# A gate product in 2x2 blocks with seven block products, its weight sums by DMA in DRAM and its operand sums by DMA in place

## The chip, the cores and the metric

The kernel runs on one core of a Trainium2 chip. The metric is the device time of one execution in microseconds, given as the median of three runs. The engines are TensorE (PE, its weight loads PEld), VectorE (DVE), ScalarE (ACT), GpSimd (POOL) and SyncE (SP); SP issues most transfers, POOL the rest, among them all transfers that add to their destination.

## What is computed

One decoder layer on 1024 tokens of width 1024 in float32. Its last two steps matter here, and the sums around them:

```python
h = h + jnp.concatenate([y_a, y_b, y_c], axis=-1) @ w_out[i]
f = jnp.square(jax.nn.relu(rms_norm(h, norm2_g[i]) @ w_ff1[i]))
h = h + f @ w_ff2[i]                                   # FF2, depth 4096
gate = jax.nn.sigmoid(rms_norm(h, norm3_g[i]) @ w_ple_gate[i])   # 1024 x 1024
h = h + gate * (p[i] @ w_ple_proj[i])
```

rms_norm multiplies by the gain g and by one root per token, R = (mean of h squared + eps)^-0.5. The kernel multiplies by g3 before the gate product and by R behind it.

## The kernel before

Activations lie with features on the 128 partitions and tokens along the free axis: h is 8 blocks n of 128 features by two halves h of 512 tokens (`h_res[n][h]`). Every float32 operand is split into a high and a low part (`split` L131 to L138: ScalarE writes hi, VectorE the rest lo), and a product of a 128 x 128 weight unit with 512 token columns is three matmuls, hi by hi, hi by lo, lo by hi (`product` L157 to L163, `run` L727).

FF1 and FF2 already go by the seven-product scheme: weights and activations are 2 x 2 blocks, A11 to A22 of the weight times B11 to B22 of (features, tokens), and products 1 to 7 use single blocks or sums of blocks on both sides. The table for the weight side (L703):

```python
OPERAND = {1: "A11", 2: "A12", 4: "A22", 5: "S1", 6: "S2", 7: "S3", 3: "S4"}
```

The sums S1 to S4 of w_ff2 are made ahead in DRAM (`w_sums`, `block_sums` L282 to L300) by copies and accumulating transfers of POOL. The sums of f are made on POOL by `token_sums` (L721) during FF1, stored in `f_dram`, and fetched again as `f` pairs.

FF2 (L919 to L998) runs over two depth chunks c, in each over the products p in the order `DOWN`, in each product over four blocks j of 128 outputs. One such step is 8 depth units x 3 = 24 matmuls into one PSUM bank; a bank is shared by the mates 1 and 2, 5 and 3, 7 and 4. VectorE then adds the bank to `u_sum` or to `h_res`. In the last chunk `finish` squares a finished h (`late_squares` L783, ScalarE) and POOL adds the squares to `S3[h]`.

The root of a half: `root_of` (L794) multiplies S3 by ones (`ms_ps`), VectorE makes the mean `ms`, POOL the power `r`, VectorE the diagonal `diag`; `spread_root` (L811) multiplies by ones (`R_ps`) and ScalarE copies R into S3's place.

The gate product (L999 to L1034) is plain. Between FF2 and it, `h3` pairs are made from h x g3 by `split`. It runs over pairs of output blocks n0, n0+1; in each pair over half 1 and then half 0; each of the 16 combinations is 8 depth units x 3 matmuls of 512 columns, the last (n = 7, half 0) in two pieces of 256. `gated` (L1006 to L1014) then does four operations on a result: multiply by R (VectorE, from PSUM), sigmoid (ScalarE), multiply by the projected embedding `pps` and add h (both VectorE), and the store: on POOL for n under 6, on SP for 6 and 7. Half 1's root is computed at the start of the gate, half 0's behind the first half-0 block.

PSUM has eight banks; the late SBUF slots are w 22, raw 4, sum 6, tmp 12, R 2 and a pool of 56 slots for h, f, u and pairs. `fetch` (L673) loads on SP. Within an engine instructions are in order; the framework's scheduler sets that order from a simulated timeline, starting from the order in which the program writes them.

Of the kernel before, what the change touches and what calls it, by code (L numbers as in the profile page):

```python
# [7 lines left out]
F32 = mybir.dt.float32  # L8
# [5 lines left out]
P = 128  # L14
# [18 lines left out]
def hybrid_block(ctx: ExitStack, tc: tile.TileContext, a: dict):  # L33
# [687 lines left out]
    def token_sums(b11, b12, b21, b22, eng, t1, t2, t3, t4):  # L721
        subtract(eng, t1, b11, b12)
        add(eng, t2, b22, t1)
        subtract(eng, t3, b22, b12)
        subtract(eng, t4, t2, b21)

    def run(bank, w, b, first, last):  # L727

# [141 lines left out]
    for i in range(FT):  # L870
        slots = iter(range(7 * i, 7 * i + 7))

        def product_up(bank, p, first, last):
            slot_no = next(slots)
            run(bank, up_pairs.pop((i, p)), hn[p], first, last)
            supply(slot_no + 1)
            if stores:
                to, t = stores.pop(0)
                nc.sync.dma_start(to, t)

        ba, bb, bc, bd = (late_bank("f_ps") for _ in range(4))
        product_up(ba, 1, True, False)
        v = late_slot("tmp", "v")
        nc.scalar.copy(v, ba)  # L884
# [27 lines left out]
        token_sums(f11, f12, f21, f22, nc.gpsimd, t1, t2, t3, t4)  # L912
        stores += [(f_dram[i, p - 1], t) for p, t in
                   ((3, f22), (1, f11), (2, f21), (5, t1), (6, t2), (7, t3), (4, t4))]
    for to, t in stores:
        nc.sync.dma_start(to, t)


    h_res = [[None, None] for _ in range(KT)]  # L919
    u_sum = [None] * 4  # L920
    h3 = [[None, None] for _ in range(KT)]
    S3 = [late_slot("R", "S3") for _ in range(2)]
    R3 = S3
    DOWN = (1, 5, 2, 3, 6, 7, 4)
    CHUNKS = FT // KC
    steps = [(c, p, j) for c in range(CHUNKS) for p in DOWN for j in range(4)]

    def f_pairs():
        for c in range(CHUNKS):
            for p in DOWN:  # L930
# [30 lines left out]
    def finish(n, h):  # L961
        late_squares(S3[h], h_res[n][h], not seen[h])
        seen[h] = True

    seen = [False, False]
    for s, (c, p, j) in enumerate(steps):
        bank = d_bank.pop((MATE[p], j)) if p in MATE else late_bank("d_ps")
        if p in (1, 5, 7):
            d_bank[p, j] = bank
        w_of.append(next(w_made, None))  # L970
        make_f(KC // 4)
        run(bank, w_of.pop(0), f_of[c, p], p not in MATE, p not in (1, 5, 7))
        last = c == CHUNKS - 1
        if p == 1:
            if c == 0:
                u_sum[j] = slot("u")
                nc.scalar.copy(u_sum[j], bank)
            else:
                add(nc.vector, u_sum[j], u_sum[j], bank)
        elif p == 6:  # L980
            subtract(nc.vector, u_sum[j], u_sum[j], bank)
            if last:
                add(nc.vector, h_res[j][1], h_res[j][1], u_sum[j])
                finish(j, 1)
                for h in range(2):
                    t = residual(j + 4, h)
                    subtract(nc.vector, t, t, u_sum[j])
        elif p in (2, 3):
            t = residual(j, p - 2)
            add(nc.vector, t, t, bank)  # L990
            if last and p == 2:
                finish(j, 0)
        else:
            h = 0 if p == 4 else 1
            t = residual(j + 4, h)
            subtract(nc.vector, t, t, bank)
            if last and p != 5:
                finish(j + 4, h)  # L998
    for n, h in [(j + 4 * i, h) for i, h in ((0, 0), (0, 1), (1, 1), (1, 0)) for j in range(4)]:  # L999
        h3[n][h] = pair("h3")  # L1000
        split(h_res[n][h], *h3[n][h], scale=g3[:, n:n + 1])


    diag = root_of(S3[1], "31")

    def gated(n, h, g_ps, c):  # L1006
        gt = late_slot("tmp", "gt")[:, c]
        nc.vector.tensor_tensor(out=gt, in0=g_ps, in1=R3[h][:, c], op=ALU.mult)
        nc.scalar.activation(gt, gt, AF.Sigmoid)
        nc.vector.tensor_tensor(out=gt, in0=gt, in1=pps[n, h][:, c], op=ALU.mult)  # L1010
        ot = late_slot("tmp", "ot")[:, c]
        nc.vector.tensor_tensor(out=ot, in0=gt, in1=h_res[n][h][:, c], op=ALU.add)
        queue = nc.sync if n >= KT - 2 else nc.gpsimd
        queue.dma_start(a["out"][n * P:(n + 1) * P, half[h]][:, c], ot)  # L1014

    pps, undone = {}, []
    for n0 in range(0, KT, 2):
        wus = [plain_units(a["w_ple_gate"][n]) for n in (n0, n0 + 1)]
        for n, h in [(n, h) for h in (1, 0) for n in (n0, n0 + 1)]:
            pps[n, h] = fetch(pp_dram[n][:, half[h]], "sum")  # L1020
            last = n == KT - 1 and h == 0

            for c in (slice(0, 256), slice(256, HT)) if last else (slice(0, HT),):
                g_ps = late_bank("g_ps")[:, c]
                product(g_ps, [(wus[n - n0][k], cols(h3[k][h], c)) for k in range(KT)])
                undone.append((n, h, g_ps, c))
                if n == 0:
                    if h == 0:
                        diag = root_of(S3[0], "30")
                    continue  # L1030
                if n == 1:
                    spread_root(diag, R3[h])
                while undone:
                    gated(*undone.pop(0))  # L1034


# [60 lines left out]
```

## Time and profile before

| | |
|---|---|
| runs | 1258.04, 1260.59, 1261.03 us; median 1260.59 |
| profiled execution | 1262.6 us, its span 1260.9 |
| mean granted TensorE clock | 0.984 |
| busy share of the span | PE 96%, PEld 82%, DVE 70%, ACT 48%, POOL 29% |
| FF2, first to last matmul | 860.2 to 1164.8 us |
| gate product | 1165.65 to 1256.06 us |

The times inside the execution count from the start of the span; 1.7 us of the profiled execution lie outside it. Rows of groups have the line, engine, operation, names (out<-in), shape and count, then busy us and mean ns, then idle time before them and what ended it. Rows in order of time begin with start and duration in us; in brackets stands the idle time before and its releaser.

### The profile page before, as it was taken

Reading aid. Unit: us, or ns where it says so; the run is one execution under the profiler, and the core shown is the slowest. Engines: PE = TensorE matmul, PEld = TensorE weight load, DVE = VectorE, ACT = ScalarE, POOL = GpSimd, SP = SyncE. Lnnn points to the kernel's source line nnn. Section 1 sums busy time; section 2 is a strip of 40 time slices with the busy share of each in tenths; the row PEclk is TensorE's granted clock in tenths of the full one; section 3 lists DMA queues with packets and bytes.
Section 4 is the critical chain, followed back from the end, with each engine's and each line's share of the span. In section 5 each row is a group of like instructions: output and inputs, shape, how many; then the busy total and the mean of one; then the engine's idle time right before and its main releaser. Section 6 shows DMA issues by size and latency. Waiting matters only on the chain.

```text
span 1260.9 us, 17509 instructions
## 1 busy us (share of the span) xinstructions
PE 1215.0 (96%) x5868; PEld 1034.1 (82%) x5868; DVE 880.7 (70%) x1324; ACT 603.8 (48%) x1167; POOL 364.2 (29%) x365
## 2 busy tenths in 40 slices
PE   9999898899999999879999999999999999999998
PEld 7898798898888878658888888888888888888887
DVE  7746886898979654676887777777755565686443
ACT  7725655666656454553334334344544344555211
POOL 2324434455323212233553453431000000122110
PEclk9999998999999999989999999999999999999999
DMA  9603257788542298689999999958956565653231
GB/s 309 211 18 117 84 158 210 167 210 159 119 114 38 67 292 226 175 221 251 269 244 255 252 244 250 252 193 302 354 179 224 183 223 170 203 166 106 76 111 51
DMA packets 118700, 234.89 MB, mean 186 GB/s; under 512 B 13105, under 2 KB 20529, under 8 KB 118353
## 3 DMA queue, kind: packets, MB, share of 16 engines
q1 hardware_dynamic: 94752, 168.08, 40.4%
q0 software_dynamic: 23856, 65.70, 23.3%
q8 instruction: 46, 0.75, 0.3%
q14 instruction: 46, 0.37, 0.1%
HBM read 176.57 MB, written 78.64 MB: 202 GB/s over the span
## 4 chain that ended last, share of the span: by engine, by line
PE 82%; DVE 8%; DMA 5%; issue 2%; ACT 1%; POOL 1%; SPq 0%; DVEq 0%; POOLq 0%; ACTq 0%
PE d_ps L731 24%; PE f_ps L731 24%; PE qkv_ps L161 3%; PE qkv_ps L162 3%; PE qkv_ps L163 3%; PE g_ps L161 2%; PE g_ps L163 2%; PE g_ps L162 2%; DVE rem L413 2%; PE av L456 2%; DMA S<-sq 2%; PE w_tr L438 1%; PE cv_ps L161 1%; DMA h_dram<-h 1%; PE cv_ps L162 1%
## 5 line engine op out<-in xcount | busy, mean ns | idle before, releaser
L135 DVE TENSOR_TENSOR w_lo<-raw,w_hi 128x512 fp32r<-128x512 f32 x268 | 244.9, 916 | 94.4 <-ACT w_hi L134 92.2
L134 ACT CAST w_hi<-raw 128x512 fp32r<-128x512 f32 x268 | 165.2, 619 | 242.6 <-PE d_ps L731 116.7
L731 PE MATMUL f_ps<-hn_hi,w_hi 128*128 128x512 f32 x448 | 176.5, 394 | 5.3 <-ACT v L884 5.3
L731 PE MATMUL f_ps<-hn_lo,w_hi 128*128 128x512 f32 x448 | 175.7, 392 | 0.0
L731 PE MATMUL f_ps<-hn_hi,w_lo 128*128 128x512 f32 x448 | 175.3, 392 | 0.0
L731 PE MATMUL d_ps<-f_hi,w_lo 128*128 128x512 f32 x448 | 174.3, 389 | 0.0
L731 PE MATMUL d_ps<-f_hi,w_hi 128*128 128x512 f32 x448 | 174.3, 389 | 0.0
L731 PE MATMUL d_ps<-f_lo,w_hi 128*128 128x512 f32 x448 | 174.3, 389 | 0.0
L731 PEld LDWEIGHTS f_ps<-hn_hi,w_hi 128*128 128x128 f32 x448 | 85.1, 190 | 23.4 <-ACT v L884 5.7
L719 POOL TENSOR_TENSOR S<-S,sq 128x512 f32<-128x512 f32 x14 | 22.6, 1614 | 273.5 <-ACT sq L788 273.5
L731 PEld LDWEIGHTS f_ps<-hn_lo,w_hi 128*128 128x128 f32 x448 | 85.1, 190 | 17.9 <-issue 0.2
L731 PEld LDWEIGHTS f_ps<-hn_hi,w_lo 128*128 128x128 f32 x448 | 85.0, 190 | 18.0
L731 PEld LDWEIGHTS d_ps<-f_hi,w_hi 128*128 128x128 f32 x448 | 84.1, 188 | 17.6
L731 PEld LDWEIGHTS d_ps<-f_lo,w_hi 128*128 128x128 f32 x448 | 84.1, 188 | 17.4
L731 PEld LDWEIGHTS d_ps<-f_hi,w_lo 128*128 128x128 f32 x448 | 84.1, 188 | 17.3
L413 DVE TENSOR_TENSOR_SCAN rem<-rem 128x128 f32<-128x128 f32 (+3 forms) x64 | 89.0, 1393 | 11.1 <-ACT rem L409 10.6
L161 PE MATMUL qkv_ps<-whi,xn_hi 128*128 128x384 f32 x256 | 92.0, 359 | 2.6 <-DVE V L138 2.6
L163 PE MATMUL qkv_ps<-whi,xn_lo 128*128 128x384 f32 x256 | 89.8, 351 | 0.0
L162 PE MATMUL qkv_ps<-wlo,xn_hi 128*128 128x384 f32 x256 | 89.8, 351 | 0.0
L135 DVE TENSOR_TENSOR f_lo<-raw,f_hi 128x512 fp32r<-128x512 f32 x112 | 77.6, 723 | 4.6 <-ACT f_hi L134 4.0
L134 ACT CAST f_hi<-raw 128x512 fp32r<-128x512 f32 x112 | 67.0, 620 | 17.9 <-DMA raw<-f_dram 13.4
L416 POOL TENSOR_TENSOR wt<-wt,rem 128x127 f32<-128x127 f32 (+4 forms) x40 | 44.3, 1109 | 107.7 <-DVE rem L413 44.9
(219 smaller groups left out, 2665.7 us busy)
## 6 DMA issues: line engine op xcount, KB each, us to landing
raw<-in_w_ff SPq DMA_DIRECT2D x160, 256.0 KB, 4.1
raw<-f_dram SPq DMA_DIRECT2D x112, 256.0 KB, 4.8
raw<-w_sums SPq DMA_DIRECT2D x64, 256.0 KB, 3.7
f_dram<-f SPq DMA_DIRECT2D x48, 256.0 KB, 4.4
f_dram<-t SPq DMA_DIRECT2D x48, 256.0 KB, 3.9
w_sums<-in_w_ff POOLq DMA_DIRECT2D x8, 1024.0 KB, 11.7
w_sums<-w_sums POOLq DMA_DIRECT2D x8, 1024.0 KB, 12.4
raw<-in_w_ff POOLq DMA_DIRECT2D x32, 256.0 KB, 5.4
```

The source lines that it names most:

```text
L134: nc.scalar.copy(hi, src)
L135: low.tensor_tensor(out=lo, in0=src, in1=hi, op=ALU.subtract)
L161: nc.tensor.matmul(ps, lh, rh, start=first and i == 0, stop=False)
L162: nc.tensor.matmul(ps, lh, rl, start=False, stop=False)
L163: nc.tensor.matmul(ps, ll, rh, start=False, stop=last and i == len(terms) - 1)
L413: nc.vector.tensor_tensor_scan(out=back, data0=back, data1=back, initial=1.0, op0=ALU.mult, op1=ALU.bypass)
L416: done = (nc.vector if on_vector else nc.gpsimd).tensor_tensor(out=wt[:, :W - 1], in0=wt[:, :W - 1], in1=rem[:, 1:W], op=ALU.mult)
L438: nc.tensor.transpose(tr[:, n:n + P], wts[i][:, kb * P:(kb + 1) * P], ident)
L456: nc.tensor.matmul(av[:, first * P:], lhs, part[:, o:o + m], start=kb == 0 and part is hi, stop=kb == 2 * g + 1 and part is lo)
L719: return eng.tensor_tensor(out=out, in0=x, in1=y, op=ALU.add)
L731: nc.tensor.matmul(bank, l, r, start=first and k == 0 and i == 0, stop=k == len(b) - 1 and i == 2, skip_group_check=True)
```

## The change

1. `w_ple_gate` comes in 2 x 2 blocks (`quad_blocks` on the host, where the arrays are laid out). Its sums S1 to S4 are made in DRAM as `g_sums`: 16 copies and 16 accumulates of 256 KB, all on POOL, behind the last `token_sums` of FF1, that is at the start of FF2.
2. FF2's second chunk takes the products in the order 1, 2, 6, 7, 4, 5, 3. Half 0 is then complete before product 5, and its root is computed inside product 5's steps; half 1 is complete with product 3, the last.
3. The activation side of the gate: for products 1, 2, 3 twelve `h3` pairs straight from h (`h3_pair`). For the sums ScalarE writes 16 scaled copies `hg` (h x g3 or h x -g3, `scale_h`), POOL adds them to each other in place by 16 transfers from SBUF to SBUF (`sum_h`), and `h3_sum` splits the results. Four sums are chained for each block j: 11 += 12, then 12 += 22, then 22 += 11, then 21 += 22, each reading what the one before left.
4. The gate product takes the products in the order 1, 2, 3, 6, 5, 7, 4, four blocks j each, 4 depth units x 3 matmuls a block; the last block of products 7 and 4 in two pieces of 256 columns. Product 2 adds to product 1's banks and 4 to 7's.
5. The epilogue: `gated` as before, with VectorE operations ahead of it for products 6, 5, 7 and 4 (`v`, `e`) and a ScalarE copy of `v` for product 1. Stores go out on POOL but for n = 6 and 7 of half 0, on SP.

```diff
+    minus_g3 = const.tile([P, KT], F32, name="minus_g3")
+    nc.vector.tensor_scalar_mul(minus_g3, g3, -1.0)
...
+    g_sums = dram.tile([4, 4, P, HT], F32, name="g_sums")
+    with tc.issue_after(summed.ins):
+        for j in range(4):
+            for to, what in ((0, "A21"), (2, "A11"), (0, "+A22"), (1, "A11"), (2, "+A21"),
+                             (1, "+S1"), (3, "A12"), (3, "+S2")):
...
+                if what[0] == "+":
+                    nc.gpsimd.dma_start(g_sums[to, j], src, accum_op=ALU.add,
+                                        max_dma_last_dim=2048)
+                else:
+                    nc.gpsimd.dma_start(g_sums[to, j], src)
...
-    DOWN = (1, 5, 2, 3, 6, 7, 4)
+    DOWN = [(1, 5, 2, 3, 6, 7, 4), (1, 2, 6, 7, 4, 5, 3)]
...
+    def scale_h(of, n, h, g):
+        t = scaled[of, n % 4] = slot("hg")
+        nc.scalar.activation(t, h_res[n][h], AF.Copy, scale=g[:, n:n + 1])
...
+    def sum_h(to, of, j):
+        nc.gpsimd.dma_start(scaled[to, j], scaled[of, j], accum_op=ALU.add)
+
+    def h3_sum(p, of, j):
+        h3[p][j] = two_parts(scaled[of, j], lambda s: slot(f"h3_{s}", F32R))
...
+        if last and p == 5:
+            if j == 1:
+                diag = root_of(S3[0], "30")
+            elif j == 3:
+                spread_root(diag, R3[0])
+        elif last and p == 3:
...
+            for n in range(3) if j == 2 else (3,) if j == 3 else ():
+                scale_h("12", n, 1, minus_g3)
+                sum_h("11", "12", n)
...
+    GATE = (1, 2, 3, 6, 5, 7, 4)
+    MATE = {2: 1, 4: 7}
...
+            for bank, c in zip(banks, cs):
+                run(bank, w, [cols(b, c) for b in h3[p]], p not in MATE, p not in (1, 7))
+                if p == 1:
+                    v_of[j] = late_slot("tmp", "v")
+                    nc.scalar.copy(v_of[j], bank)
+                elif p == 2:
+                    gated(j, 0, bank, late_slot("tmp", "gt"), c)
+                elif p == 6:
+                    subtract(nc.vector, v_of[j], v_of[j], bank)
+                elif p == 5:
+                    e_of[j] = late_slot("tmp", "e")
+                    add(nc.vector, e_of[j], bank, v_of[j])
+                    t = late_slot("tmp", "gt")
+                    add(nc.vector, t, d_bank.pop((3, j))[0], e_of[j])
+                    gated(j, 1, t, t, c)
+                elif p == 7:
+                    t = e_of[j][:, c]
+                    add(nc.vector, t, bank, t)
+                    gated(j + 4, 1, t, t, c, -1.0)
+                elif p == 4:
+                    t = v_of[j][:, c]
+                    add(nc.vector, t, bank, t)
+                    gated(j + 4, 0, t, t, c, -1.0)
+            if p == 1:
+                if j == 1:
+                    diag = root_of(S3[1], "31")
+                elif j == 3:
+                    spread_root(diag, R3[1])
+                h3_pair(2, j + 4, 0)
+                sum_h("12", "22", j)
+            elif p == 2:
+                h3_pair(3, j + 4, 1)
+                sum_h("22", "11", j)
+            elif p == 3:
+                h3_sum(6, "22", j)
+                sum_h("21", "22", j)
+            elif p == 6:
+                h3_sum(5, "11", j)
+            elif p == 5:
+                h3_sum(7, "12", j)
+            elif p == 7:
+                h3_sum(4, "21", j)
```

What the change moves shows in the order of instructions on three engines. On POOL, from the end of FF2 on, before: S3 sums of squares, the two roots (L169), and stores.

```order
L719 TENSOR_TENSOR S3_1911_8635<-S3_1911_8635,sq_2627_11353 128x512
L719 TENSOR_TENSOR S3_1910_8634<-S3_1910_8634,sq_2634_11393 128x512
L719 TENSOR_TENSOR S3_1910_8634<-S3_1910_8634,sq_2641_11433 128x512
L719 TENSOR_TENSOR S3_1910_8634<-S3_1910_8634,sq_2648_11473 128x512
L169 TENSOR_TENSOR r_2684_11575<-ms_2683_11573,mhalf_109 128x4
L719 TENSOR_TENSOR S3_1910_8634<-S3_1910_8634,sq_2649_11501 128x512
L1014 DMA out_T<-ot_2704_11664 128x512
L1014 DMA out_T<-ot_2706_11671 128x512
L169 TENSOR_TENSOR r_2711_11708<-ms_2710_11706,mhalf_109 128x4
L1014 DMA out_T<-ot_2717_11746 128x512
L1014 DMA out_T<-ot_2719_11753 128x512
```

And now, the last twelve of the sums in place (L996) with the last sum of squares and half 1's root (L171):

```order
L996 DMA hg_2657_11505<-hg_2676_11571 128x512
L996 DMA hg_2660_11511<-hg_2656_11503 128x512
L721 TENSOR_TENSOR S3_1911_8670<-S3_1911_8670,sq_2677_11599 128x512
L996 DMA hg_2676_11571<-hg_2661_11513 128x512
L996 DMA hg_2658_11507<-hg_2678_11602 128x512
L996 DMA hg_2671_11559<-hg_2660_11511 128x512
L996 DMA hg_2661_11513<-hg_2657_11505 128x512
L171 TENSOR_TENSOR r_2696_11665<-ms_2695_11663,mhalf_109 128x4
L996 DMA hg_2678_11602<-hg_2662_11515 128x512
L996 DMA hg_2672_11561<-hg_2661_11513 128x512
L996 DMA hg_2662_11515<-hg_2658_11507 128x512
L996 DMA hg_2673_11563<-hg_2662_11515 128x512
```

The last sums of squares, which stood side by side, now have transfers between them, and the root r_2696 stands behind the twelfth of sixteen transfers; the stores follow the last.

On TensorE, where half 1's root is spread (R_ps), before: behind the second block of the gate (n = 1), which is complete.

```order
L163 MATMUL g_ps_2701_11632<-h3_hi_2670_11544,w_lo_2697_11600 128x512
L161 MATMUL g_ps_2701_11632<-h3_hi_2672_11548,w_hi_2696_11599 128x512
L162 MATMUL g_ps_2701_11632<-h3_lo_2673_11549,w_hi_2696_11599 128x512
L163 MATMUL g_ps_2701_11632<-h3_hi_2672_11548,w_lo_2697_11600 128x512
L813 MATMUL R_ps_2702_11657<-diag_2685_11577,ones_88 128x512
L161 MATMUL g_ps_2708_11676<-h3_hi_2650_11504,w_hi_2687_11581 128x512
L162 MATMUL g_ps_2708_11676<-h3_lo_2651_11505,w_hi_2687_11581 128x512
```

Now it stands inside the first block of product 2, between its eighth and ninth matmul:

```order
L733 MATMUL g_ps_2682_11611<-h3_lo_2699_11670,w_hi_2709_11703 128x512
L733 MATMUL g_ps_2682_11611<-h3_hi_2698_11669,w_lo_2710_11704 128x512
L733 MATMUL g_ps_2682_11611<-h3_hi_2705_11695,w_hi_2709_11703 128x512
L733 MATMUL g_ps_2682_11611<-h3_lo_2706_11696,w_hi_2709_11703 128x512
L815 MATMUL R_ps_2712_11721<-diag_2697_11667,ones_88 128x512
L733 MATMUL g_ps_2682_11611<-h3_hi_2705_11695,w_lo_2710_11704 128x512
L733 MATMUL g_ps_2682_11611<-h3_hi_2713_11724,w_hi_2709_11703 128x512
L733 MATMUL g_ps_2682_11611<-h3_lo_2714_11725,w_hi_2709_11703 128x512
```

It moved from a place between two blocks, behind 48 matmuls of the gate (two plain blocks of 24), to one inside a block, behind 56.

On VectorE, the end of the program, before: the two pieces of the last block, three operations each (L1008 times R, L1010 times pps, L1012 plus h).

```order
L1008 TENSOR_TENSOR gt_2802_12229<-g_ps_2801_12204,S3_1910_8634 128x256
L1010 TENSOR_TENSOR gt_2802_12229<-gt_2802_12229,raw_2800_12202 128x256
L1012 TENSOR_TENSOR ot_2803_12233<-gt_2802_12229,h_2313_10117 128x256
L1008 TENSOR_TENSOR gt_2805_12261<-g_ps_2804_12236,S3_1910_8634 128x256
L1010 TENSOR_TENSOR gt_2805_12261<-gt_2805_12261,raw_2800_12202 128x256
L1012 TENSOR_TENSOR ot_2806_12265<-gt_2805_12261,h_2313_10117 128x256
```

Now, from the first piece's addition on (L721 with g_ps as input adds the bank, L1065 times R, L1067 times pps, L721 with h as input adds h):

```order
L721 TENSOR_TENSOR v_2711_11719<-g_ps_2848_12274,v_2711_11719 128x256
L721 TENSOR_TENSOR v_2693_11656<-v_2693_11656,h_2287_10050 128x512
L721 TENSOR_TENSOR v_2711_11719<-g_ps_2849_12275,v_2711_11719 128x256
L1065 TENSOR_TENSOR v_2711_11719<-v_2711_11719,S3_1910_8669 128x256
L1067 TENSOR_TENSOR v_2704_11693<-v_2704_11693,raw_2867_12382 128x512
L1065 TENSOR_TENSOR v_2711_11719<-v_2711_11719,S3_1910_8669 128x256
L1067 TENSOR_TENSOR v_2711_11719<-v_2711_11719,raw_2868_12402 128x256
L721 TENSOR_TENSOR v_2704_11693<-v_2704_11693,h_2300_10101 128x512
L721 TENSOR_TENSOR v_2711_11719<-v_2711_11719,h_2313_10152 128x256
L1067 TENSOR_TENSOR v_2711_11719<-v_2711_11719,raw_2868_12402 128x256
L721 TENSOR_TENSOR v_2711_11719<-v_2711_11719,h_2313_10152 128x256
```

The operations of the last three results are interleaved; behind the addition of the last bank (g_ps_2849) stand eight others.

More of the change, by code (lines that the diff above doesn't have):

```diff
@@ L990, in hybrid_block @@
             add(nc.vector, t, t, bank)
-            if last and p == 2:
-                finish(j, 0)
+            if last:
+                finish(j, p - 2)
         else:
@@ L996, in hybrid_block @@
             subtract(nc.vector, t, t, bank)
-            if last and p != 5:
+            if last and p != 7:
                 finish(j + 4, h)
[L999 to L1034, printed above, removed]
+        if last and p == 5:
[4 more added lines that the diff above has]
+        elif last and p == 3:
+            for n in (2 * j, 2 * j + 1) if j < 2 else ():
+                h3_pair(1, n, 0)
+            if j == 1:
+                for n in range(4):
+                    scale_h("11", n, 0, g3)
+                for n in range(4):
+                    scale_h("22", n + 4, 1, g3)
+            elif j == 2:
+                for n in range(4):
+                    scale_h("21", n + 4, 0, minus_g3)
+            for n in range(3) if j == 2 else (3,) if j == 3 else ():
+                scale_h("12", n, 1, minus_g3)
+                sum_h("11", "12", n)
```

56 lines of the change are left out of this document (49 added, 7 removed).

## The prediction

> **What bounds the kernel now.** I read first the busy time by stretches, then the groups of instructions by line and shape in the gate product, then the end in order of time. The first view has for each stretch its length and, for each engine, busy us and (x) instructions; then the granted TensorE clock, the DMA share and GB/s.
>
> ```profile
> core 0: us, PE busy (x) PEld busy (x) DVE busy (x) ACT busy (x) POOL busy (x), PEclk, DMA share, GB/s
> 820.00:960.00 140.00, 140.00 (x620) 115.95 (x619) 97.45 (x140) 69.06 (x120) 18.05 (x12) 1.00 0.74 255
> 960.00:1120.00 160.00, 160.00 (x708) 132.53 (x707) 98.25 (x153) 73.78 (x126) 8.36 (x5) 1.00 0.58 194
> 1129.00:1165.00 36.00, 36.00 (x162) 29.82 (x160) 26.15 (x34) 18.98 (x32) 11.37 (x8) 1.00 0.34 103
> 1165.00:1256.00 91.00, 91.00 (x429) 75.68 (x427) 39.92 (x60) 15.89 (x26) 10.21 (x15) 1.00 0.23 82
> ```
>
> TensorE is busy in every microsecond of FF2 and of the gate product, at full clock. Both stages are as long as their matmuls. What one matmul costs is its distance to the next, not its listed duration, since matmuls overlap:
>
> ```profile
> L731 PE MATMUL d_ps<-f_hi,w_hi x448: 389/389/390, 860.2 to 1164.2; 128*128 128x512 f32 x150
> L161 PE MATMUL g_ps<-h_hi,w_hi 128*128 128x512 f32 x120 | 47.7, 398 | 0.0
> L161 PE MATMUL g_ps<-h_hi,w_hi 128*128 128x256 f32 x16 | 4.5, 283 | 0.0
> 1250.50 0.28 PE L161 MATMUL g_ps<-h_hi,w_hi 128*128 128x256 f32 x1
> 1250.62 0.28 PE L162 MATMUL g_ps<-h_lo,w_hi 128*128 128x256 f32 x1
> ```
>
> The first row runs from its first to its last start over 447 turns of three matmuls: (1164.2 - 860.2)/1341 = 0.2267 us for 512 columns. The last two rows give 0.12 us for 256. The gate has 3 x 120 of the one and 3 x 16 of the other.
>
> ```profile
> 1255.78 0.28 PE L163 MATMUL g_ps<-h_hi,w_lo 128*128 128x256 f32 x1
> 1256.10 0.42 DVE L1008 TENSOR_TENSOR gt<-g_ps,S 128x256 f32<-128x256 f32 x1 [1.08 <-PE g_ps L163]
> 1256.55 0.42 ACT L1009 ACTIVATE gt<-gt 128x256 f32<-128x256 f32 x1 [2.46 <-DVE gt L1008]
> 1257.00 0.43 DVE L1010 TENSOR_TENSOR gt<-gt,raw 128x256 f32<-128x256 f32 x1 [0.48 <-ACT gt L1009]
> 1257.46 0.42 DVE L1012 TENSOR_TENSOR ot<-gt,h 128x256 f32<-128x256 f32 x1
> ```
>
> After the last matmul (its end is 1256.06) come four short operations, done at 1257.88, and the store, up to 1260.9. The tail is 4.8 us.
>
> **The change, part by part.** *Matmuls.* Seven products of 4 blocks x 4 depth units x 3 make 336 matmuls for 384. In both kernels 48 of them have 256 columns (now the last block of products 7 and 4), so 360 full ones become 312. 48 x 0.2267 = **-10.9 us**. The two root computations (eight ms_ps and two R_ps matmuls each in the trace) only move, half 0's into FF2. FF2 keeps its blocks; their order in the second chunk costs nothing, as each loads the same tiles.
>
> *Tail.* In the listing of the end, nine VectorE operations stand behind the last bank of results where three stood: seven of 256 columns and two of 512, since the last three blocks are finished interleaved. Back to back an operation of 512 columns takes 0.60 us:
>
> ```profile
> 1180.53 0.69 DVE L1012 TENSOR_TENSOR ot<-gt,h 128x512 f32<-128x512 f32 x1
> 1181.14 0.68 DVE L1008 TENSOR_TENSOR gt<-g_ps,S 128x512 f32<-128x512 f32 x1
> 1181.74 0.68 DVE L135 TENSOR_TENSOR w_lo<-raw,w_hi 128x512 fp32r<-128x512 f32 x1
> ```
>
> The same overlap of 0.09 makes 0.34 of the 0.43 for 256 (an estimate). 7 x 0.34 + 2 x 0.60 = 3.6 us, with 0.13 around them, for 1.82 now: +1.9 if VectorE is caught up. It may not be: from the first subtraction of product 6 it has 52 full and 16 half operations, 52 x 0.60 + 16 x 0.34 = 36.6 us, in the 41.2 us that TensorE takes from there (156 full, 48 half matmuls). At 89% load it can be one or two operations late, and chained halves take 0.46, not 0.34. Bounds +1.9 and +4; I take **+2.5 us**.
>
> *Work beside TensorE.* 12 more weight pairs, 16 scaled copies, 16 splits of sums for 4 pairs saved, and 20 more epilogue operations:
>
> ```profile
> L137 ACT ACTIVATE h_hi<-h,c_g 128x512 fp32r<-128x512 f32 x15 | 10.1, 715 | 0.0
> L134 ACT CAST f_hi<-raw 128x512 fp32r<-128x512 f32 x102 | 60.8, 620 | 12.9 <-DMA raw<-f_dram 8.5 <-PE d_ps L731 2.7
> L135 DVE TENSOR_TENSOR f_lo<-raw,f_hi 128x512 fp32r<-128x512 f32 x102 | 68.9, 705 | 4.3 <-ACT f_hi L134 3.6 <-DMA f_dram<-t 0.3
> ```
>
> ScalarE: 12 x 0.72 + 28 x 0.62 = 26 us on top of 34.9 in the 127 us from 1129 to 1256; VectorE: 24 x 0.70 + 20 x 0.69 = 31 on top of 66.1 (4 to 5 us more where a split waits). Neither fills the 116 us that are left, so I take 0; if the splits of one product came late in a row, VectorE's excess is bounded by the rival below.
>
> *Weight sums.* 16 copies and 16 accumulates of 256 KB go out on POOL at the start of FF2, where POOL has nothing else. For rates I take the same two steps of FF2's sums: the first two rows are the DMA share and GB/s of 100 to 180 us with the copies in 2 us slices, the third is 310 to 393 us with accumulates:
>
> ```profile
> DMA  0000000299098700000929000000000009090009
> GB/s 0 0 0 0 0 0 0 66 459 524 13 267 240 245 29 0 0 4 0 426 98 524 8 0 0 0 0 0 0 0 0 0 0 524 0 524 12 0 0 524
> GB/s 208 204 204 206 203 209 179 9 8 0 0 0 49 139 162 181 218 196 239 219 207 209 92 0 0 0 126 248 131 8 123 67 0 63 0 0 0 0 0 8
> ```
>
> A copy at 524 GB/s is 0.50 us of all DMA engines and an accumulate at 204 is 1.28: 16 x 1.78 = 28.5 us. Free in 820 to 960 are 0.26 x 140 = 36 us, to 1120 another 67. The sums are used only in the gate. Hidden, 0 us; if loads of the first FF2 products are held up instead, TensorE waits at most a part of it (rival).
>
> *Operand sums.* Sixteen in-place accumulates on POOL near the end of FF2, four chained ones per block. The listing of POOL has the half-1 root (r_2696) behind twelve of them. The same operation exists in the kernel before, under a DMA share near 1:
>
> ```profile
> L790 POOL DMA_DIRECT2D S<-sq x14: 843/857/892, 457.7 to 548.1; - x14
> DMA to landing us min/median/max: 3.4/5.2/8.0
> raw<-in_w_ple_gate SPq DMA_DIRECT2D x16, 256.0 KB, 2.6
> raw<-in_w_ff SPq DMA_DIRECT2D x160, 256.0 KB, 4.1
> 1166.48 1.03 POOL L169 TENSOR_TENSOR r<-ms,mhalf 128x4 f32<-128x4 f32 x1 [3.74 <-DVE ms L801]
> L806 DVE TENSOR_TENSOR diag<-ident,r 128x512 f32<-128x512 f32 x2 | 2.5, 1232 | 0.0
> L813 PE MATMUL R_ps<-diag,ones 128*128 128x512 f32 x4 | 2.0, 592 | 0.0
> 1165.00 0.79 PE ms_ps L798 x8
> ```
>
> Call L the time from issue to landing, T the end of FF2. Product 3's first block of the last chunk (24 matmuls a block, 5.44 us, four of them) ends at T - 16.3; its addition, scaling and the way to POOL take some 2.9, so the first sum goes out at T - 13.4. Five landings stand in a row before r_2696 (the waits are between links of a chain, and POOL issues in order), then one issue of 0.86, the root 1.03, the diagonal some 0.7 to 1.2 and handovers: the diagonal is ready at about T + 5L - 9.7. TensorE meets R_ps behind 56 matmuls of the gate and the ms_ps: T + 56 x 0.2267 + 0.79 = T + 13.5. It waits only if **L exceeds 4.6 us**. The gate's DMA share is 0.34 and less, plain loads take 2.6 there and 4.1 under load; the median 5.2 less that 1.5 is 3.7, and I add 0.5 because sums overlap each other: L = 4.2, ready at T + 11.3, 2.2 us to spare, **0 us**. Bounds 3.4 (min) and 8.0 (max of one). Each microsecond over 4.6 costs five.
>
> The Trainium skill ("DMA: Bandwidth & Descriptors", section "Anatomy of one DMA — SWDGE (gpsimd) path") fits 2.0 us plus bytes over 436e3 for a transfer issued by GpSimd, 2.6 us for 256 KB, by which the diagonal would be ready at T + 3.3 with ten to spare. The row contradicts it for accumulates: none of 14 landed under 3.4.
>
> Sum: -10.9 + 2.5 = **-8.4 us**, against the profiled execution's own 1262.6 us: 1254.2. That execution lies 2.0 over the median shown, so the median should be **1252.2 us**.
>
> **Rivals.** *Slower: the chain of sums takes the root with it.* One mechanism: POOL's sums land late (L over 4.6), r_2696 is behind them, R_ps stands in TensorE's order ahead of the rest of product 2. At L = 6 the diagonal comes at T + 20.3, 6.8 us late. A wait like this costs again through the clock:
>
> ```profile
> 548.86 0.79 PE L731 MATMUL f_ps<-hn_hi,w_hi 128*128 128x512 f32 x1 [5.32 <-ACT v L884]
> 551.16 0.63 PE L731 MATMUL f_ps<-hn_hi,w_lo 128*128 128x512 f32 x1
> 551.58 0.63 PE L731 MATMUL f_ps<-hn_hi,w_hi 128*128 128x512 f32 x1
> 548.00:552.00 4.00, 3.14 (x7) 2.48 (x8) 4.00 (x8) 4.00 (x9) 1.08 (x2) 0.60 0.97 295
> ```
>
> After 5.32 us idle the granted clock was 0.60 and matmuls stood 0.42 us apart for some eight: 8 x 0.2 = 1.6 us. The splits of the last sums, two landings later still, hold VectorE's queue in front of product 6's subtractions, for which the banks of product 5 wait: some 3 us. Together +11.4, net +3.0: 1263.6 for the median. It decides from L = 5.4 (the 8.4 gained, less those 4.6, is 3.8, over five), and needs the loaded median on lightly loaded queues: 0.10.
>
> The Trainium skill ("TensorE: Matmul & The Clock Gate", section "Part 1: The HAM clock gate (the "warmup" mystery)") says that the clock halves after an idle window of about 3.4 us until some 3.4 us of work have passed. The rows agree with it in kind, with 0.60 over the slice; by it the loss would be 1.7 us for 1.6.
>
> *Weight sums against FF2's loads.* The 28.5 us fall into a stretch at share 0.74, and FF2's second product has its f pairs only just ahead. A stall of 5 us leaves -3.4: 1257.2. For it: the accumulates' 204 GB/s; against it: the average free share. 0.15.
>
> *VectorE sets the pace of products 5, 7 and 4.* With 89% load, any slip of 3 us more than I allow ends in the tail: -5.4, 1255.2. 0.13.
>
> That fewer matmuls are not saved is ruled out by the listing, which has 336.
>
> **How the numbers follow.** Forecast 0.62, the rivals 0.15, 0.13 and 0.10. Likeliest: 1252.2, with its own range 1250.5 to 1253.5 by the tail's bounds (+1.9 to +4) and 0.8 for the spread of the runs. Reaching over the two middle cases and part of the way to the slower one, and a little below for a tail that overlaps better, the range is 1249.5 to 1259.0. A change under 0.3% (3.8 us) cannot be told from none. Faster: 0.62, the VectorE rival's 0.13 almost whole (0.11) and a third of the weight-sum one (0.05): 0.78. Within: the remaining 0.10 + 0.02, so 0.12. Slower: 0.10.
>
> **What would show it.** From the end of FF2 to the last matmul 79 us for 91, with no TensorE wait at R_ps (10.9 saved, and 0.79 + 2 x 0.43 of half 0's root now inside FF2, 304 us before and 306 after); landings of hg under 4.6 us; a tail of 7 us. I am wrong if TensorE waits for diag, for a split h3 or for f pairs at the start of FF2, or if more than 4 us of VectorE work follow the last matmul.

## The result

| | before | changed |
|---|---|---|
| median, 20 runs each | 1259.04 us (1253.44 to 1262.52) | 1261.76 us (1257.46 to 1266.06) |
| profiled execution | 1262.6, span 1260.9 | 1259.36, span 1257.7 |

The ratio is 1.0023, with a 95% interval of 1.0012 to 1.0034: a gain of 8.4 us was forecast and 2.7 us were lost. Measured against the 0.3% that the prediction took as its limit, that is no change; by the interval it is a small loss.

The list of TensorE's waits from 560 us on, which was empty before, has four entries now (what waited, for what, us in total, times, longest):

```profile
PE d_ps L733 <- ACT f_hi L136: 7.1, 2, 6.0
PE f_ps L733 <- DVE f L721: 0.9, 1, 0.9
PE R_ps L815 <- DVE diag L808: 0.6, 1, 0.6
PE d_ps L733 <- DVE f_lo L137: 0.2, 1, 0.2
```

7.3 us are in FF2 (d_ps), for pairs of f; the root (R_ps) costs 0.6; f_ps belongs to FF1, ahead of the change. FF2's own rows, first and last start of the first and third of its matmul forms:

```profile
L733 PE MATMUL d_ps<-f_hi,w_hi x448: 389/389/793, 852.5 to 1170.4; 128*128 128x512 f32 x150
L733 PE MATMUL d_ps<-f_hi,w_lo x448: 387/389/628, 852.9 to 1170.9; 128*128 128x512 f32 x150
```

Called FF2's length below: 1170.9 - 852.5 = 318.4 us, for 304.4 before. The start of FF2 by stretches, in the changed kernel:

```profile
core 0: us, PE busy (x) PEld busy (x) DVE busy (x) ACT busy (x) POOL busy (x), PEclk, DMA share, GB/s
860.00:868.00 8.00, 8.00 (x37) 6.64 (x36) 5.56 (x9) 4.05 (x8) 5.25 (x11) 1.00 0.88 297
868.00:876.00 8.00, 8.00 (x37) 6.64 (x36) 0.00 (x0) 0.00 (x0) 5.36 (x9) 1.00 1.04 355
876.00:884.00 8.00, 6.63 (x28) 4.91 (x28) 1.99 (x3) 2.14 (x4) 4.57 (x6) 1.00 1.03 252
...
900.00:908.00 8.00, 2.21 (x10) 1.50 (x8) 3.27 (x5) 2.38 (x5) 2.44 (x3) 0.82 1.10 277
908.00:916.00 8.00, 7.71 (x17) 5.09 (x18) 4.25 (x7) 3.03 (x6) 0.00 (x0) 0.54 1.05 324
```

The weight sums are issued from 859.9 to 905.0 us. From 868 to 876 VectorE and ScalarE do nothing at all; ScalarE's next cast waits 11 us for a load of weights:

```profile
877.94 0.62 ACT L136 CAST w_hi<-raw 128x512 fp32r<-128x512 f32 x1 [11.01 <-DMA raw<-in_w_ff]
```

TensorE lives on what was made ahead, stops in 876 to 884 and for 6.0 us up to 908. The median landing times (from issue to landing, the last number) of the issues from 856 to 916 us say why. First the changed kernel:

```profile
g_sums<-in_w_ple_gate POOLq DMA_DIRECT2D x24, 256.0 KB, 7.4
raw<-f_dram SPq DMA_DIRECT2D x15, 256.0 KB, 15.9
raw<-in_w_ff SPq DMA_DIRECT2D x8, 256.0 KB, 15.9
g_sums<-g_sums POOLq DMA_DIRECT2D x8, 256.0 KB, 8.7
```

and the same stretch before:

```profile
raw<-f_dram SPq DMA_DIRECT2D x29, 256.0 KB, 5.1
...
raw<-in_w_ff SPq DMA_DIRECT2D x8, 256.0 KB, 4.8
```

A load takes three times as long, and 15 loads of f are made where 29 were. Around the long wait ScalarE gets one load of f every 2.0 us:

```profile
907.55 0.62 ACT L136 CAST f_hi<-raw 128x512 fp32r<-128x512 f32 x1 [3.29 <-DMA raw<-f_dram]
909.56 0.62 ACT L136 CAST f_hi<-raw 128x512 fp32r<-128x512 f32 x1 [1.39 <-DMA raw<-f_dram]
911.55 0.62 ACT L136 CAST f_hi<-raw 128x512 fp32r<-128x512 f32 x1 [1.38 <-DMA raw<-f_dram]
```

The first block of a product needs eight pairs, one for every three matmuls, that is one in 3 x 0.2267 = 0.68 us at full pace; the other three blocks use the same eight again. So it is in a product's first block that the lead is used up. Both stops are there, at the seventh pair of the second and of the third product (before FF2's 115th and 211th matmul). After the long one the matmuls restart slowly:

```profile
908.22 0.79 PE L733 MATMUL d_ps<-f_hi,w_hi 128*128 128x512 f32 x1 [6.02 <-ACT f_hi L136]
...
910.23 0.29 PEld L733 LDWEIGHTS d_ps<-f_hi,w_hi 128*128 128x128 f32 x1 [0.78 <-ACT f_hi L136]
...
914.53 0.63 PE L733 MATMUL d_ps<-f_hi,w_hi 128*128 128x512 f32 x1
914.96 0.56 PE L733 MATMUL d_ps<-f_lo,w_hi 128*128 128x512 f32 x1
915.36 0.39 PE L733 MATMUL d_ps<-f_hi,w_lo 128*128 128x512 f32 x1
```

The granted clock there, third number from the end:

```profile
912.00:913.00 1.00, 1.00 (x4) 0.81 (x3) 0.69 (x1) 0.17 (x1) 0.00 (x0) 0.50 1.06 404
```

Fourteen of them take 7.14 us where 14 x 0.2267 = 3.2 would do: 4.0 us more, behind a wait of 6.0. Two things make them up. The granted clock is 0.50 up to 915, and where the pairs are there the matmuls stand 0.43 us apart instead of 0.23 (914.53 to 914.96): 14 x 0.2 = 2.8 us. The other 1.2 us are more waiting for pairs, as in the weight load at 910.23; the list of waits leaves it out, since by its modelled end the matmul before ran almost up to it (0.63 us from 909.54).

The gate and its end went as forecast. The operand sums, from the view of their tile:

```profile
L996 POOL DMA_DIRECT2D hg<-hg x16: 859/902/1564, 1157.7 to 1194.7; - x16
...
DMA to landing us min/median/max: 3.3/4.5/6.2
```

The last matmul and the end of VectorE, in order of time:

```profile
1250.18 0.28 PE L733 MATMUL g_ps<-h_hi,w_lo 128*128 128x256 f32 x1
...
1253.85 0.42 DVE L1067 TENSOR_TENSOR v<-v,raw 128x256 f32<-128x256 f32 x1
1254.31 0.42 DVE L721 TENSOR_TENSOR v<-v,h 128x256 f32<-128x256 f32 x1
```

From the start of FF2's last matmul to that of the gate's last: 1250.18 - 1170.9 = 79.3 us, for 91.2 before. From there to the end of the span: 7.5 us, for 5.1. So, of the two profiled executions: up to FF2 -7.7 us, FF2 +14.0, gate -11.9, tail +2.4, together -3.2. The -7.7 is no part of the change: the order of instructions up to there is the same on every engine but for one VectorE operation that makes a small constant, and the kernels below with the same front began FF2 anywhere from 852.5 to 860.9 us.

### The profile page after: what moved, and what is told of

It is laid out like the page before. It is cut to its first block, busy times and chain, and to the rows that moved or that the text cites. A ratio compares the mean times of both kernels' runs of the same rounds, so it can differ in the third digit from the quotient of the medians.

```text
span 1257.7 us, 17658 instructions
## 1 busy us (share of the span) xinstructions
PE 1203.4 (96%) x5820; PEld 1022.3 (81%) x5820; DVE 903.7 (72%) x1374; ACT 628.1 (50%) x1212; POOL 400.6 (32%) x416
## 4 chain that ended last, share of the span: by engine, by line
PE 75%; DMA 9%; DVE 9%; issue 3%; POOL 1%; ACT 1%; SPq 0%; POOLq 0%; ACTq 0%; DVEq 0%
PE f_ps L733 22%; PE d_ps L733 20%; PE g_ps L733 5%; PE qkv_ps L163 3%; DMA raw<-in_w_ff 3%; PE qkv_ps L164 3%; PE qkv_ps L165 3%; DVE rem L415 2%; PE av L458 2%; PE o_ps L163 2%; PE cv_ps L163 2%; PE o_ps L164 1%; PE o_ps L165 1%; PE cv_ps L165 1%; PE cv_ps L164 1%
## 5 line engine op out<-in xcount | busy, mean ns | idle before, releaser
L137 DVE TENSOR_TENSOR w_lo<-raw,w_hi 128x512 fp32r<-128x512 f32 x280 | 250.5, 898 | 104.4 <-ACT w_hi L136 103.8
L136 ACT CAST w_hi<-raw 128x512 fp32r<-128x512 f32 x280 | 172.1, 618 | 233.8 <-PE d_ps L733 96.7
L721 POOL TENSOR_TENSOR S<-S,sq 128x512 f32<-128x512 f32 x14 | 21.9, 1561 | 225.6 <-ACT sq L790 225.6
```

The costliest lines, as they stand in the source:

```text
L136: nc.scalar.copy(hi, src)
L137: low.tensor_tensor(out=lo, in0=src, in1=hi, op=ALU.subtract)
L721: return eng.tensor_tensor(out=out, in0=x, in1=y, op=ALU.add)
```

## The experiments

Every kernel ran beside the kernel before on the same chip; its median there was 1258.27 to 1258.62 us. The column on waits has TensorE's waits for f pairs as the profile lists them; the one on pairs counts the casts of f_hi in the 50 us from FF2's first matmul.

| kernel | median us | ratio, 95% interval | FF2 us | listed waits in FF2 us | f pairs in 50 us |
|---|---|---|---|---|---|
| before | 1259.04 | | 304.4 | 0 | 27 |
| changed | 1261.76 | 1.0012 to 1.0034 | 318.4 | 7.3 | 12 |
| e1 sums spread later | 1249.34 | 0.9907 to 0.9952 | 306.3 | 0 | 27 |
| e2 sums later, bunched | 1252.14 | 0.9916 to 0.9958 | 306.3 | 0 | 27 |
| e3 no sums | 1251.42 | 0.9902 to 0.9952 | 306.2 | 0 | 27 |
| e5 before, with the sums | 1264.17 | 1.0021 to 1.0057 | 309.7 | 2.8 | 13 |
| e6 copies in short rows | 1253.25 | 0.9942 to 0.9976 | 309.1 | 1.7 | 14 |
| e8 copies now, rest later | 1254.02 | 0.9935 to 0.9975 | 308.2 | 1.3 | 21 |
| e10 the same, short rows | 1250.98 | 0.9927 to 0.9967 | 306.3 | 0 | 24 |
| e9 copies in FF1, rest now | 1250.69 | 0.9910 to 0.9959 | 307.0 | 0.2 | 16 |
| e11 32 long copies | 1252.26 | 0.9923 to 0.9960 | 307.0 | 0.2 | 15 |
| e12 32 short copies | 1250.46 | 0.9918 to 0.9956 | 306.3 | 0 | 15 |
| e7 e1, additions on POOL | 1252.50 | 0.9925 to 0.9967 | 306.3 | 0 | |

**e1, the sums spread over later steps.** The transfers are the same; a 128x4 addition on POOL that reads what a step of FF2 wrote keeps two of them behind that step.

```diff
-    with tc.issue_after(summed.ins):
-        for j in range(4):
...
+        if s >= 16 and SUM_STEPS:
+            seen_on = u_sum[j] if p in (1, 6) else t
+            mark = small.tile([P, 4], F32, tag="mark", name=name("mark"), bufs=1)
+            with tc.issue_after(add(nc.gpsimd, mark, seen_on[:, :4], seen_on[:, :4]).ins):
+                for _ in range(2):
+                    sum_step(*SUM_STEPS.pop(0))
```

> The changed kernel with its 32 weight-sum transfers moved: two behind each of FF2's steps 17 to 32 (a 128x4 addition on POOL, which reads what the step wrote, holds them back) instead of all at the start of FF2. Theory A (the sums hold up the loads of FF2's first products, 7.3 us of waits and some 5 us of lowered clock): no TensorE wait for f pairs, FF2 306 us from first to last matmul instead of 318.5, median 1249.4 us. Theory B (the longer FF2 comes from its new product order and from half 0's root inside it): FF2 stays at 318, median 1261.8. Theory C (the transfers cost what they cost wherever in FF2 they go): waits move to 950 to 1040 us, FF2 312 to 318, median 1256 to 1262.

Theory A holds: no wait for f, FF2 306.3 where 306 was expected, and a gain whose interval leaves out 1. That the median (1249.34 for 1249.4) fits so closely is luck: its interval is 5.7 us wide, and e2 and e3 below, with the same FF2, have 1252.14 and 1251.42. Theory C falls: the same 32 transfers, at a DMA share up to 0.98, cost FF2 nothing there. The busiest of the stretches with the sums in e1, TensorE full:

```profile
980.00:1020.00 40.00, 40.00 (x178) 33.14 (x177) 24.33 (x38) 17.08 (x29) 13.53 (x24) 1.00 0.98 309
```

and the only wait of TensorE from 840 us on:

```profile
PE R_ps L815 <- DVE diag L808: 0.3, 1, 0.3
```

FF2 is 1.9 us longer than before. That is half 0's root, which now stands in it (0.79 + 2 x 0.43 = 1.7 by the prediction's rows).

**e2, all 32 behind one step.**

```diff
-        if s >= 16 and SUM_STEPS:
-                for _ in range(2):
+        if s >= 16 and SUM_STEPS:
+                for _ in range(32):
```

> As the run before, but all 32 transfers in one go behind step 17 of FF2 (about 950 us). Theory A with a price set by how full the DMA engines are: the share there was 0.45 to 0.55 before against 0.8 to 0.9 at FF2's start, and pairs are further ahead, so waits of 0 to 4 us, median 1249 to 1255. If it is the bunching that costs and not the place: waits of 7 us again, median 1261. Theory B: 1261.8.

No wait at all. The place decides, not the bunching: by step 17 the pairs are far enough ahead. The medians of e1, e2 and e3 cannot be told apart by their intervals.

**e3, no sums.**

```diff
-                src = w_block("w_ple_gate", of, j) if of[0] == "A" else g_sums[int(of[1]) - 1, j]
+                src = w_block("w_ple_gate", of if of[0] == "A" else ("A11", "A12", "A21", "A22")[int(of[1]) - 1], j)
```

> The changed kernel without the 32 weight-sum transfers; the gate's products with a sum take a plain block of w_ple_gate in its place, so the output is another. Theory A: FF2 306 us, no waits for f pairs, median 1249.4, the same as with the transfers spread. Theory B: 1261.8.

FF2 306.2 us: theory B falls, and e1 pays nothing for its transfers. One doubt is left. With the transfers, the order of SP's loads and of the casts on ScalarE and VectorE moved too in e1, e2 and e3; e12 below settles it.

**e5, the sums alone, added to the kernel before.** `w_half` takes the block out of the old layout, so the sources have rows of 2 KB.

```diff
+    g_sums = dram.tile([4, 4, P, HT], F32, name="g_sums")
+    with tc.issue_after(summed.ins):
...
+                src = (g_sums[int(of[1]) - 1, j] if of[0] == "S"
+                       else w_half(of, j))
```

> The kernel before with the same 32 transfers added at the same place (start of FF2), their result unused. Theory A: waits for f pairs of some 7 us with a lowered clock behind them, FF2 317 us instead of 304.4, median 1259.0 + 12.4 = 1271.4. Theory B: 1259.0.

The direction of theory A, but not its size: 5.3 us more of FF2 instead of 12.4, and 1264.17 us where 1271.4 was expected. Of the differences between the two, the rows of the copies were the one that could be tested by itself: 16 KB in the changed kernel, 2 KB here.

**e6, the changed kernel with its copies in short rows.**

```diff
-                    nc.gpsimd.dma_start(g_sums[to, j], src)
+                    nc.gpsimd.dma_start(g_sums[to, j], src, max_dma_last_dim=2048)
```

> The changed kernel with the 16 copies of the weight sums written in rows of 2 KB (128x512) as the loads and accumulates are, instead of 16 KB (16x4096); every engine's order is unchanged, the place too. In the changed kernel no load landed and VectorE and ScalarE did nothing from 868 to 876 us, while the copies ran; the kernel before with the same transfers in short rows lost 5 us, not 12. Theory A1 (the amount of transfer time at that place decides): FF2 318 us, median 1261.8. Theory A2 (the long rows of the copies keep SP's loads out): FF2 309 to 312, median 1252 to 1255.

As A2 had it: 1253.25 for 1261.76 us, FF2 309.1 for 318.4. One argument of 16 transfers is worth nine microseconds of FF2. It does not work through the amount: from 856 to 916 us the packets of POOL's queue took 58.6% of the DMA engines' time in the changed kernel and 57.2% in e6. In e6 the stretch in which the changed kernel's VectorE and ScalarE stood still has work, at a higher rate:

```profile
868.00:876.00 8.00, 8.00 (x37) 6.61 (x36) 1.94 (x3) 2.03 (x4) 4.21 (x8) 1.00 1.04 394
```

**e8, e9 and e10, one kind of transfer at a time.** e8 leaves the copies at FF2's start and spreads the accumulates; e9 spreads the copies over FF1 and leaves the accumulates; e10 is e8 with short rows.

```diff
+    with tc.issue_after(summed.ins):
+        for j, to, what in SUM_STEPS:
+            if what[0] != "+":
+                sum_step(j, to, what)
```

> The changed kernel with the 16 copies where they are, at the start of FF2, and the 16 accumulates moved behind FF2's steps 17 to 32, one each. A1: 8 of 28.5 us of transfer time stay at the start; waits of 0 to 2 us, FF2 306 to 309, median 1249.5 to 1252. A2: the copies do the harm, waits of 4 us or more remain at about 880 to 910 us, FF2 312 or more, median 1255 or more.

In e9 one copy goes out behind each round of token sums in FF1:

```diff
+        if i < FT - 1:
+            with tc.issue_after(summed.ins):
+                for _ in range(2 if i < 1 else 1):
+                    sum_step(*COPIES.pop(0))
```

> The changed kernel with the copies spread over FF1 (one behind each of its rounds of token sums) and the 16 accumulates at the start of FF2. A1: 20.5 of 28.5 us stay there, waits of 4 to 6 us, median 1256 to 1260. A2: waits of at most 3 us, FF2 306 to 310, median 1249.5 to 1254.

And e10 against e8:

```diff
-            nc.gpsimd.dma_start(g_sums[to, j], src)
+            nc.gpsimd.dma_start(g_sums[to, j], src, max_dma_last_dim=2048)
```

> The kernel with the 16 copies at the start of FF2 and the accumulates spread later (1254.02 us), the copies now in rows of 2 KB; order unchanged. A2: the remaining 1.3 us of waits with their clock go, FF2 306, median 1249.5 to 1251.5. A1: 1254.

Neither theory holds in both: e8's FF2 is as A1 had it (308.2; its median lies above A1's range), e9 is as A2 had it. The copies alone (e8) wait 1.3 us, the accumulates alone (e9) 0.2, both together 7.3. They are not additive. e10 has no wait: short rows take e8's away (FF2 306.3 for 308.2; the intervals of the two medians overlap).

**e11 and e12, 32 plain copies in long and in short rows.** With e6 and the changed kernel these make four that have one order of instructions on every engine and differ in the form of these transfers only.

```diff
-                if what[0] == "+":
-                    nc.gpsimd.dma_start(g_sums[to, j], src, accum_op=ALU.add,
-                                        max_dma_last_dim=2048)
-                else:
-                    nc.gpsimd.dma_start(g_sums[to, j], src)
+                nc.gpsimd.dma_start(g_sums[to, j], src)
```

e12 has `max_dma_last_dim=2048` in that last line as well.

> The changed kernel with the 16 accumulates of the weight sums replaced by plain copies in rows of 16 KB too, at the same place (32 copies; the sums are then wrong, so the output is another). Every engine's order is unchanged. A copy takes less of the DMA engines than an accumulate (0.50 us against 1.28), so all 32 take 16 us instead of 28.5. A1 (transfer time decides): no more than the accumulates alone cost (0.2 us of waits): FF2 306 to 307, median 1249.5 to 1251. A2 (long rows keep SP's loads out as long as they run): waits of 5 us or more around 880 to 900 us, FF2 314 or more, median 1257 or more. Between them (both add to one backlog of loads, of which some 15 us are covered by loads made ahead): waits of 1 to 4 us, median 1251.5 to 1257.

> As the run before with all 32 copies in rows of 2 KB. A1: as the run before, 1249.5 to 1251 (the copies in short rows ran at about the same rate). A2: no waits, FF2 306, median 1249.5 to 1251, several us less than the run before.

0.2 us of waits with long rows, none with short ones; FF2 307.0 and 306.3, the medians not to be told apart. So long rows do not shut loads out for as long as they run: A2 falls in its strong form. e12 also settles the doubt about the order: it has that of the changed kernel on every engine, SP's loads included, and no wait in FF2. The order is not the cause.

The last column of the table orders all twelve but e8. Pairs made in 50 us fall from 27 to 15 without a wait that matters; at 14 and 13 TensorE waits 1.7 and 2.8 us, at 12 it waits 7.3. That copies and accumulates, and the rows of the copies, draw on one stock of pairs, and that the row length decided because the changed kernel stood at its end, is read from this order; no run tests it by itself. The places of the waits say more. At the second product's seventh pair the three kernels with 16 KB rows at FF2's start wait (the changed one and e8 1.3 us each, e11 0.2), and none with short rows does. At the third product's seventh or eighth pair the four with accumulates there wait: the changed one 6.0 us, e5 2.8, e6 1.7, e9 0.2.

Why 16 KB rows delay the loads was not measured by itself. Single loads took up to 23.8 us to land in e11 (issued from 860 to 910 us) and up to 15.3 in e12. The Trainium skill ("DMA: Bandwidth & Descriptors", section "Queues, rings and completion order") says that a DMA engine takes turns between queues by packets, not by bytes, which would give the queue with long rows the larger share. The runs agree with that in direction (14 pairs against 12, 24 against 21); the pairs of e11 and e12 (15 and 15) do not show it.

**e7, VectorE relieved at the end.** On e1, the last addition of products 5 and 7 goes to POOL.

```diff
-        add(nc.vector, t, t, h_res[n][h][:, c])
+        add(plus, t, t, h_res[n][h][:, c])
...
-                    gated(j, 1, t, t, c)
+                    gated(j, 1, t, t, c, plus=nc.gpsimd)
...
-                    gated(j + 4, 1, t, t, c, -1.0)
+                    gated(j + 4, 1, t, t, c, -1.0, plus=nc.gpsimd)
```

> The kernel with the spread transfers (1249.34 us) and the last addition of products 5 and 7, plus h, on POOL instead of VectorE: eight operations of 512 columns and one in two halves. Theory D (VectorE, busy 29.7 of the last 30 us of the gate, brings a backlog into the tail): its 4.8 us less leave it caught up, the tail falls from 7.2 to about 5.5, median 1247.6. Rival: nine VectorE operations stand behind the last bank as before, the tail stays at 7.2 and the median at 1249.3; or POOL's additions slow VectorE and it gets longer.

Theory D falls, and the second rival holds in the trace. From the last matmul's start to the end are 1250.7 - 1242.0 = 8.7 us, for 7.5 in e1. The medians of e7 and e1 (1252.50 and 1249.34) cannot be told apart by their intervals. Some of VectorE's groups in 25 us near the end (1219 to 1244 in e1, 1222 to 1247 in e7), first e1, then e7 (mean ns behind the comma):

```profile
L1072 DVE TENSOR_TENSOR e<-e,S 128x512 f32<-128x512 f32 x3 | 2.0, 680 | 0.0
L1074 DVE TENSOR_TENSOR e<-e,raw 128x512 f32<-128x512 f32 x3 | 2.0, 682 | 0.0
L721 DVE TENSOR_TENSOR e<-g_ps,e 128x512 f32<-128x512 f32 x3 | 2.0, 682 | 0.0
```

```profile
L1072 DVE TENSOR_TENSOR e<-e,S 128x512 f32<-128x512 f32 x3 | 3.4, 1149 | 0.1
L1074 DVE TENSOR_TENSOR e<-e,raw 128x512 f32<-128x512 f32 x3 | 3.2, 1067 | 0.8 <-ACT e L1073 0.7
L721 DVE TENSOR_TENSOR e<-g_ps,e 128x512 f32<-128x512 f32 x3 | 2.1, 684 | 0.1
```

and from e7 in order of time some operations of POOL and VectorE:

```profile
1225.28 1.28 POOL L721 TENSOR_TENSOR gt<-gt,h 128x512 f32<-128x512 f32 x1 [0.39 <-DVE gt L1074]
1225.29 1.83 DVE L1074 TENSOR_TENSOR e<-e,raw 128x512 f32<-128x512 f32 x1
1227.04 0.68 DVE L721 TENSOR_TENSOR e<-g_ps,e 128x512 f32<-128x512 f32 x1
1227.20 1.29 POOL L721 TENSOR_TENSOR e<-e,h 128x512 f32<-128x512 f32 x1 [0.63 <-DVE e L1074]
1227.75 1.28 DVE L1072 TENSOR_TENSOR e<-e,S 128x512 f32<-128x512 f32 x1
...
1229.73 0.69 DVE L1074 TENSOR_TENSOR e<-e,raw 128x512 f32<-128x512 f32 x1 [0.70 <-ACT e L1073]
```

Operations with both inputs in SBUF became longer where POOL added beside them. The two shown end 0.56 and 0.54 us after POOL's addition does (1227.12 for 1226.56, 1229.03 for 1228.49), whatever their own start, as if the one had waited for the other. The one at 1229.73, with no addition beside it, took its usual 0.69. The one at 1227.04, which reads a PSUM bank, kept its 0.68 with a POOL addition beside most of it. So what VectorE was spared in count came back in length.

## Why the prediction was wrong

*Matmuls:* right. 10.9 us less, and half 0's root moved: the gate is 11.9 us shorter where -10.9 - 1.7 + 0.6 = -12.0 was to be expected with the wait measured.

*Tail:* the number is right, +2.4 us for +2.5, and so is the engine: VectorE ends 4.55 us after the last matmul's start for 2.10 before. The load behind it was not. The prediction gave VectorE the 41.2 us that TensorE takes from product 6's first subtraction on. In the trace that subtraction came 6.2 us after its block was done, behind splits (TensorE's row, then VectorE's):

```profile
1208.94 0.39 PE L733 MATMUL g_ps<-h_hi,w_lo 128*128 128x512 f32 x1
1214.31 1.31 DVE L137 TENSOR_TENSOR w_lo<-raw,w_hi 128x512 fp32r<-128x512 f32 x2
1215.52 0.70 DVE L718 TENSOR_TENSOR v<-v,g_ps 128x512 f32<-128x512 f32 x1
```

VectorE had 34.7 us left, was busy in nearly all of them and had caught up to half a microsecond when the last matmul came. That it did is in part luck.

*Operand sums:* nearly right. L was taken as 4.2 us and measured 4.5; the limit was put at 4.6 and R_ps waited 0.6 us (0.3 to 1.1 in the experiments). By the prediction's formula 4.5 leaves 0.7 us to spare, so 1.3 us are missing in the chain: from the first transfer's issue (1157.71) to the twelfth's (1182.81) its five links took 25.1 us, 5.0 each with the waits between them. The slower rival, which needed L = 6, did not come about.

*Work beside TensorE:* right for TensorE, which waits for none of it in the gate (0.2 and 0.3 us in e6 and e12); VectorE fell behind by it, as the tail shows.

*Weight sums: the step that failed.* "Hidden, 0 us" cost 12.1 us (14.0 of FF2 less the 1.9 of the root): 7.3 of listed waits, 2.8 for the lowered clock, and 2.0 of late pairs that the list leaves out. e1, with these transfers moved, gives 1249.34 us, 0.9929 of the kernel before; the sum had said -8.4 of 1260.6, which is 0.9933. So the other terms hold; that the two ratios are so close is luck, as said above.

It failed first by the stretch over which the free share was taken. The prediction set 28.5 us of transfers against 36 free in 140 us. The transfers do not spread over 140 us: POOL issues them in 45, from 7.4 us after FF2's first matmul on. In the kernel before, where FF2 begins at 860.2, these are 868 to 913 us:

```profile
868.00:876.00 8.00, 8.00 (x37) 6.64 (x36) 5.79 (x9) 4.27 (x8) 0.16 (x1) 1.00 0.83 269
876.00:884.00 8.00, 8.00 (x37) 6.60 (x36) 3.74 (x6) 4.79 (x9) 0.00 (x0) 1.00 0.76 257
884.00:892.00 8.00, 8.00 (x37) 6.63 (x36) 7.65 (x13) 5.84 (x11) 0.00 (x0) 1.00 0.88 303
892.00:900.00 8.00, 8.00 (x37) 6.64 (x36) 6.56 (x11) 5.63 (x10) 0.00 (x0) 1.00 1.05 402
900.00:908.00 8.00, 8.00 (x37) 6.63 (x36) 6.30 (x11) 4.75 (x9) 0.00 (x0) 1.00 1.06 404
908.00:916.00 8.00, 8.00 (x37) 6.61 (x36) 3.55 (x6) 1.87 (x3) 0.00 (x0) 1.00 0.81 306
```

Free are 8 x (0.17 + 0.24 + 0.12) = 4 us up to 908 and at most 1.5 in the last row. Some 23 had to come out of FF2's lead. The 28.5 was low as well: by the packets of POOL's queue the transfers took 58.6% of the 60 us from 856 to 916, 35 us, beside the loads.

The place alone does not give the price. e9 and e11 press 23.5 us each, counted in the same way, into the same stretch and pay 0.7 us of FF2; the lead covers them. e6 has all 32 transfers at that place and pays 2.8 us; its median, 1253.25, lies in the forecast's range. The other 9.3 us hang on the 16 KB rows of the copies, of which the prediction says nothing: it priced a copy by its rate alone. That the price rises so steeply because the lead runs out is argued from the column of pairs.

*The rivals:* "weight sums against FF2's loads" (0.15) was what happened, with the right place and the right victim, f pairs of the first products. Its price of 5 us was less than half of 12.1: it took the wait for 5 instead of 9.3 and left out the clock, although the rows on that stood two paragraphs above, for the other rival. There 1.6 us were put on an idle time of 5.32, for eight matmuls at half clock; here fourteen ran so, while the pairs came singly, and it was 2.8.

*The signs:* of the prediction's signs of being wrong three came true: TensorE waited for f pairs, it waited 0.6 us for diag, and 4.3 us of VectorE work, where 4 was the limit, followed the last matmul (1250.46 to 1254.73). The first is the one that cost the gain.

## What to carry to other kernels

Set a new transfer against the free share of the microseconds in which its queue will issue it, not against the stage's mean, and ask how much the stage has made ahead by then; past that lead a listed wait costs more than itself, by the late pairs behind it and, after a long one, by the clock (7.3 us became 12.1 here; in e6, at full clock, 1.7 became 2.8). Work that no one needs for 250 us is not free at the moment at which it can first be issued: tie it to a step later on. In this kernel the form of a transfer, the length of its rows, weighed nearly as much as its place (9.3 us against 12.1). Before moving elementwise work to POOL, look at whether VectorE's operations beside it read SBUF twice.

## What was not expected of the hardware

16 copies of 256 KB in rows of 16 KB instead of 2 KB, order and place unchanged, made FF2 9.3 us longer (318.4 against 309.1) beside 16 accumulates and 1.9 us (308.2 against 306.3) without them. With 32 copies and no accumulates it was 0.7 us (307.0 against 306.3).

VectorE's operations of 512 columns on two SBUF inputs took 1.28 and 1.83 us with a POOL addition beside them, against 0.68 without, and ended some 0.55 us after it; with one input in PSUM they stayed at 0.68. The Trainium skill ("SBUF — State Buffer", section "SBUF: two separate sides") says that a VectorE operation with two SBUF inputs and a GpSimd operation that reads SBUF exclude each other for their whole duration; the rows of e7 agree.

Executions of one kernel spread over 9 us (before: 1253.44 to 1262.52), and in the profiles much of that lies ahead of FF2, whose start moves by 8 us between kernels with the same front. A single profiled execution of the changed kernel was 3.2 us shorter than that of the kernel before while its median was 2.7 us longer; only the stage rows showed which was which.
